# Loading the sinks and the identity after the first activations in a streaming encoder step

## The chip, the cores and the metric

The kernel runs on one core of one Trainium2 chip. The metric is the time of one execution on the device in microseconds (us), lower is better. Before the change three runs gave 2082.37, 2082.21 and 2081.52 us, with a median of 2082.21 us.

## The reference

The program computes one inference step of a small hybrid encoder. The input is a prompt of 2048 tokens and a sample of 32 tokens, both with 1024 features. Layer 0 is a gated DeltaNet layer. Layer 1 is a sliding-window attention layer with a learned sink for each head, and both share one K and V. All arithmetic is in float32. What matters for the start of the program is the first projection:

```python
def delta_layer(x, conv_buf, s0, w_in, conv_w, a_log, dt_bias, norm_w, w_out, ln_g, ln_b):
    proj = x @ w_in                                   # 1024 -> 4096 + 16 features
    qkv, new_buf = causal_conv(proj[..., :CONV_DIM], conv_buf, conv_w)
    a_in = proj[..., CONV_DIM + A_VW:CONV_DIM + A_VW + A_HEADS]
    b_in = proj[..., CONV_DIM + A_VW + A_HEADS:]
    ...

def sink_softmax(s, sinks):                           # in layer 1 only
    sk = sinks.astype(jnp.float32)[..., None, None]
    m = jnp.maximum(s.max(-1, keepdims=True), sk)
    p = jnp.exp(s - m)
    return p / (p.sum(-1, keepdims=True) + jnp.exp(sk - m))
```

The sinks enter in the attention of layer 1, the second half of the program. The identity matrix is an operand of the transposes on TensorE, of which the first stands behind the first projections.

## The kernel before, in words

**Stages.** `program` (L2273) runs the parts one after the other: `P1` is the input projection of layer 0 with its short convolution, `Delta` the recurrence, `O1` the output projection with its layer norm, `P2` the projections of layer 1, `Attention` the rest. `make_consts` (L2426) runs ahead of all of them and fills constants that several parts use.

**How a projection is done.** A float32 operand is split into two parts of a shorter format: `hi` is a rounded copy (a cast on ACT), `lo` is the raw value less `hi` (a subtraction on DVE or POOL). A product takes three matmuls: hi by hi (L79), lo activations by hi weights (L80), hi activations by lo weights (L81). Activations come transposed in five blocks of 416 tokens (`NB`, `TB`), and one block has eight slices `k` of 128 features. Weights come in blocks of 128 output features.

**The first block.** `P1.__init__` loads `wab_raw`, the weights of 16 small gate features, on ACT's DMA queue, and then the activations (L136). Block 0 comes in four pieces `q` of two slices each, 128x832, 416 KB. Pieces 0 and 2 go through SP's queue, 1 and 3 through ACT's. Blocks 1 to 4 come in two pieces of four slices each, 128x1664, 832 KB. Piece by piece ACT casts to `act_hi` (L70) and DVE subtracts to `act_lo` (L71). The raw pieces lie in four buffers (two under each of two tags), so that a later piece of the same tag can only be loaded when DVE has subtracted an earlier one. Between blocks 0 and 1 the program text asks for the first two weight blocks (`fetch_weights`, L48, `split_fetched`, L55 and L56). There is one buffer for raw weights, so the second is loaded when the first has been split.

**What follows.** `P1.qkv` (L150) takes each activation block in turn: sixteen gate matmuls (L166 with `act_hi`, L168 with `act_lo`, in order of `k`), then the 48 matmuls of the two weight blocks. The gate rows are transposed with the identity (L174).

**What sets the order.** In this part the program text doesn't set the order of the instructions on an engine. A scheduler of the build does, with a time model of its own, and it also gives each DMA, in the order in which it places them, one of eight completion semaphores, DMAHW0 to DMAHW7. SP's and ACT's queues share the eight. A DMA that gets a semaphore waits until the earlier DMA with that semaphore has landed. Each engine works strictly through its own list: an instruction that waits holds everything behind it, and DMA issues on ACT stand in the same list as ACT's casts. Later stages are written under `manual_schedule`, where the text's own order holds.

Of the kernel before, what the change touches and what calls it, by code (L numbers as in the profile page):

```python
# [36 lines left out]
def new_pool(tc, es, name, bufs=1, space=None, side=None):  # L37
    kw = {"reuse_waits": "tile"}
    if side is not None:
        kw["side"] = side  # L40
    if space is not None:
        kw["space"] = space
    return es.enter_context(tc.tile_pool(name=name, bufs=bufs, **kw))
# [16 lines left out]
def split_weights(nc, pool, src, sub):  # L60

    return split_fetched(nc, pool, fetch_weights(nc, pool, src), sub)


def split_acts(nc, res, b, raws, sub):

    h = res.tile([128, KC, TB], F32R, tag=f"act_hi{b}", name=f"act_hi{b}")
    l = res.tile([128, KC, TB], F32R, tag=f"act_lo{b}", name=f"act_lo{b}")
    for s, raw in raws:
        nc.scalar.copy(h[:, s, :], raw)  # L70
        sub.tensor_tensor(out=l[:, s, :], in0=raw, in1=h[:, s, :], op=ALU.subtract)  # L71
    return h, l
# [25 lines left out]
class P1:  # L98
# [4 lines left out]
    def __init__(self, tc, left, right, mid, I, O, T, G):  # L103
        self.tc, self.nc, self.I, self.O, self.T, self.G = tc, tc.nc, I, O, T, G
        nc = tc.nc
        self.resl = new_pool(tc, left, "p1_resl", 1, side="left")
        self.wp = new_pool(tc, left, "p1_w", 2, side="left")
        self.ppl = new_pool(tc, left, "p1_psl", 2, PSUM, side="left")
        self.resr = new_pool(tc, right, "p1_resr", 1, side="right")
        self.big = new_pool(tc, mid, "p1_big", 2, side="right")  # L110
        self.one = one = new_pool(tc, mid, "p1_one", 1, side="right")
        self.ppr = new_pool(tc, right, "p1_psr", 4, PSUM, side="right")
        self.pt = new_pool(tc, mid, "p1_pt", 2, PSUM, side="right")
        self.turn = 0
        self.convw = one.tile([128, 24, 4], F32, tag="convw", name="convw")
        self.convs = one.tile([128, 24, 3], F32, tag="convs", name="convs")
        self.convo = one.tile([128, 24, 6], F32, tag="convo", name="convo")
        self.sel = one.tile([128, 4, 128], F32, tag="sel", name="sel")
        self.nwh = self.resl.tile([128, 1], F32, tag="nwh", name="nwh")
        raw = one.tile([128, KC, 16], F32, tag="th", name="wab_raw")  # L120
        wab = one.tile([128, KC, 48], F32R, tag="parts", name="wab")
        nc.scalar.dma_start(raw[:], I["w_ab"])
        nc.scalar.copy(wab[:, :, 0:16], raw[:])
        nc.vector.tensor_tensor(out=wab[:, :, 32:48], in0=raw[:], in1=wab[:, :, 0:16], op=ALU.subtract)
        nc.gpsimd.memset(wab[:, :, 16:32].bitcast(F32), 0.0)
        self.wab = wab
        self.x = []
        for b in range(NB):
            if b == 1:
                self.w0 = [split_weights(nc, self.wp, I["w_in"][i], (nc.vector, nc.gpsimd)[i]) for i in range(2)]  # L130
            raws = []
            step = 2 if b == 0 else 4
            for q in range(KC // step):
                raw = self.big.tile([128, step, TB], F32, tag="Ry"[q % 2], name="act_raw")
                s = slice(q * step, q * step + step)
                (nc.sync if q % 2 == 0 else nc.scalar).dma_start(raw[:], I["xT"][b][:, s, :])  # L136
                raws.append((s, raw[:]))
            self.x.append(split_acts(nc, self.resr if b < 3 else self.resl, b, raws, nc.vector))
        nc.sync.dma_start(self.convw[:], I["conv_w"])
        nc.sync.dma_start(self.convs[:], I["conv_state"])  # L140
        nc.sync.dma_start(self.nwh[:], I["norm_w"])
        nc.scalar.mul(self.nwh[:], self.nwh[:], 0.5)
        nc.sync.dma_start(self.sel[:], I["sel"])

    def ps(self):
        self.turn += 1
        return (self.ppl if self.turn % 3 == 0 else self.ppr).tile([128, 512], F32, tag="ps", name="ps")
# [2278 lines left out]
def make_consts(tc, I, pool):  # L2426
    nc = tc.nc
    G = {}
    G["ident"] = pool.tile([128, 128], F32, tag="ident", name="ident")
    nc.sync.dma_start(G["ident"][:], I["ident"])  # L2430
    raw = pool.tile([128, 12], F32, tag="sinks", name="sinks")
    for i in range(2):
        nc.sync.dma_start(raw[i * 64:i * 64 + 64, 0:8], I["sinks"][i].partition_broadcast(64))
    for i in range(4):
        nc.sync.dma_start(raw[i * 32:i * 32 + 32, 8:12], I["sinks_s"][i].partition_broadcast(32))
    G["sinks"] = pool.tile([128, 12, 2], F32, tag="twice", name="twice")
    nc.vector.tensor_copy(G["sinks"][:], raw[:].unsqueeze(2).to_broadcast([128, 12, 2]))
    for name in ("hn", "eq", "ekd", "egl", "ngc"):
        G[name] = pool.tile([128, NTT, H], F32, tag=name, name="t_" + name)
    return G  # L2440
# [135 lines left out]
```

## Time and profile before

| | |
|---|---|
| median of three runs | 2082.21 us (2081.52 to 2082.37) |
| the profiled execution | 2085.37 us |
| its span, first to last instruction | 2083.6 us |
| PE (TensorE matmul) busy | 2025.9 us, 97% of the span |
| DVE, ACT, POOL busy | 1481.4, 993.3, 917.7 us |
| first matmul starts | 11.79 us into the span |

The profiled execution is 1.77 us longer than its span, which is what lies before the first and after the last instruction, and 3.16 us longer than the median run. In the rows of the profile PE is TensorE's matmuls, PEld its weight loads, ACT is ScalarE, DVE is VectorE, POOL is GpSimd. SPq and ACTq are the DMA issues of the two queues. In a row of the timeline the first number is the start in us from the span's start and the second the time it took, x2 stands for several merged instructions, and square brackets give the idle time of the engine before it with what ended it. In a row of stretches (windows) stand the length, busy time and instruction count of each engine, the granted clock, the share of time that the 16 DMA engines were busy, and their rate.

### The profile page before, as it was taken

To read this page: it belongs to the slowest core of one execution; us is meant where nothing else is said; L and a number is where in the kernel's file an instruction comes from. 1 tells how busy PE (TensorE), PEld (TensorE's weight loads), DVE (VectorE), ACT (ScalarE), POOL (GpSimd) and SP (SyncE) were. 2 spreads that over 40 slices of the span, in tenths; PEclk is the share of its full clock that TensorE was granted. 3 is DMA by queue.
4 is the path that set the end of the run, shared out by engine and by line. 5 is a ranking of instruction groups with operands and counts; after the bars stand their busy time and mean duration, and the time that the engine had idled before them with its cause. 6 is when DMAs were issued, how large, how long until landed. Compare 5 with 4: busy or idle time off the path is not lost.

```text
span 2083.6 us, 36939 instructions
## 1 busy us (share of the span) xinstructions
PE 2025.9 (97%) x13518; PEld 1856.4 (89%) x13518; DVE 1481.4 (71%) x2580; ACT 993.3 (48%) x2445; POOL 917.7 (44%) x1248
## 2 busy tenths in 40 slices
PE   7999999999999999999989998999989998999998
PEld 5999999999999999999888887899989997777775
DVE  4477666675556778888987897877878755666665
ACT  4354444446532266777763222534634445555552
POOL 0322213222222157777860113386255523566665
PEclk9999999999999999999999999899999999999999
DMA  5132333236756645555864999888767679434321
GB/s 209 29 96 81 100 112 103 92 98 201 215 162 200 190 134 175 166 170 166 302 226 117 270 244 258 264 249 292 261 217 239 202 211 305 112 107 112 102 73 66
DMA packets 355542, 360.82 MB, mean 173 GB/s; under 512 B 157585, under 2 KB 280241, under 8 KB 355345
## 3 DMA queue, kind: packets, MB, share of 16 engines
q1 hardware_dynamic: 348880, 344.03, 53.8%
q10 hardware_dynamic: 6480, 14.44, 2.0%
q8 instruction: 106, 1.74, 0.3%
q14 instruction: 76, 0.61, 0.1%
HBM read 235.54 MB, written 134.06 MB: 177 GB/s over the span
## 4 chain that ended last, share of the span: by engine, by line
PE 79%; DMA 8%; DVE 6%; issue 2%; POOL 2%; ACT 1%; SPq 1%; DVEq 0%; ACTq 0%; POOLq 0%
PE ps L79 12%; PE ps L81 12%; PE ps L80 11%; PE ot L1133 3%; PE ot L1134 3%; PE ot L1135 3%; PE S L2026 2%; PE ot L2059 2%; PE tr L2041 2%; PE X L1684 2%; PE X L1682 2%; PE X L1683 2%; PE g L695 1%; DMA w_raw<-in_b_w 1%; PE ks L846 1%
## 5 line engine op out<-in xcount | busy, mean ns | idle before, releaser
L79 PE MATMUL ps<-act_hi,w_hi 128*128 128x416 f32 x1280 | 455.2, 356 | 0.4 <-ACT w_hi L55 0.4
L81 PE MATMUL ps<-act_hi,w_lo 128*128 128x416 f32 x1280 | 450.3, 352 | 0.0
L80 PE MATMUL ps<-act_lo,w_hi 128*128 128x416 f32 x1280 | 448.2, 350 | 0.0
L79 PEld LDWEIGHTS ps<-act_hi,w_hi 128*128 128x128 f32 x1280 | 240.3, 188 | 4.5 <-ACT w_hi L55 0.7
L80 PEld LDWEIGHTS ps<-act_lo,w_hi 128*128 128x128 f32 x1280 | 240.7, 188 | 3.1
L81 PEld LDWEIGHTS ps<-act_hi,w_lo 128*128 128x128 f32 x1280 | 240.2, 188 | 3.2
L209 DVE SCALAR_TENSOR_TENSOR y<-R,convw,y 128x2083 f32<-128x2083 f32 x72 | 182.9, 2541 | 62.5 <-ACT y L206 46.7
L56 POOL TENSOR_TENSOR w_lo<-w_raw,w_hi 128x1024 fp32r<-128x1024 f32 x25 | 71.3, 2854 | 329.8 <-ACT w_hi L55 302.5
L729 POOL TENSOR_TENSOR tm<-L,Tt 128x60 f32<-128x60 f32 (+19 forms) x365 | 134.3, 368 | 80.6 <-issue 39.6
L1860 POOL TENSOR_TENSOR P<-e,sm 128x384 f32<-128x384 f32 (+2 forms) x128 | 102.3, 820 | 119.5 <-DVE sm L1850 113.3
L731 POOL TENSOR_TENSOR Tt<-Tt,tm 128x60 f32<-128x60 f32 (+19 forms) x365 | 138.5, 380 | 28.6
L1846 ACT ACTIVATE e<-S,nm 128x193 f32<-128x193 f32 (+2 forms) x260 | 104.6, 415 | 96.4 <-DVE nm L1841 57.6
L1355 DVE TENSOR_TENSOR w_lo<-w_raw,w_hi 128x512 fp32r<-128x512 f32 x132 | 139.0, 1069 | 10.7 <-ACT w_hi L1367 5.4
L305 ACT COPY R<-ps 128x416 f32<-128x416 f32 (+1 forms) x144 | 60.3, 442 | 106.8 <-PE ps L81 91.6
L1510 ACT ACTIVATE o<-X 128x416 f32<-128x416 f32 x80 | 41.4, 518 | 131.3 <-PE X L1684 128.7
L1133 PE MATMUL ot<-wo,g_hi 128*128 128x512 f32 x256 | 103.7, 405 | 0.0
L1134 PE MATMUL ot<-wo,g_hi 128*128 128x512 f32 x256 | 100.8, 394 | 0.0
L1135 PE MATMUL ot<-wo,g_lo 128*128 128x512 f32 x256 | 100.8, 394 | 0.0
L1367 ACT CAST w_hi<-w_raw 128x512 fp32r<-128x512 f32 x129 | 76.6, 615 | 18.3 <-POOL w_raw L1498 9.5
L215 DVE SCALAR_TENSOR_TENSOR y<-th,y 128x2083 f32<-128x2083 f32 x24 | 55.8, 2327 | 36.5 <-ACT th L213 36.5
L1841 DVE TENSOR_REDUCE nm<-S 128x4 f32<-128x772 f32 (+3 forms) x66 | 60.5, 917 | 15.2 <-PE S L2026 15.2
L213 ACT ACTIVATE th<-y 128x2083 f32<-128x2083 f32 x24 | 46.7, 1947 | 47.0 <-DVE y L209 43.7
(369 smaller groups left out, 5229.0 us busy)
## 6 DMA issues: line engine op xcount, KB each, us to landing
w_raw<-in_b_w SPq DMA_DIRECT2D x60, 512.0 KB
w_raw<-in_w_in SPq DMA_DIRECT2D x40, 512.0 KB
act_raw<-s_hT SPq DMA_DIRECT2D x64, 208.0 KB
s_rows<-o SPq DMA_DIRECT2D x50, 208.0 KB
k<-s_k SPq DMA_DIRECT2D x17, 512.0 KB
E<-s_E SPq DMA_DIRECT2D x17, 512.0 KB
s_hT<-hT SPq DMA_DIRECT2D x65, 128.0 KB
s_bq<-s_rows SPq DMA_DIRECT2D x40, 208.0 KB
```

What stands on the lines that cost most here:

```text
L79: nc.tensor.matmul(ps, hi[:, k, :], xh[:, k, :], start=(k == 0), stop=False)
L80: nc.tensor.matmul(ps, hi[:, k, :], xl[:, k, :], start=False, stop=False)
L81: nc.tensor.matmul(ps, lo[:, k, :], xh[:, k, :], start=False, stop=(k == KC - 1))
L209: nc.vector.scalar_tensor_tensor(out=y[:], in0=R[:, j:j + W], scalar=self.convw[:, i, j:j + 1], in1=y[:], op0=ALU.mult, op1=ALU.add)
L729: P.tensor_tensor(out=tm[:n, i0 - k:, :w], in0=L[:n, i0:, j:j + 1].to_broadcast(sh), in1=Tt[:n, j:j + 1, :w].to_broadcast(sh), op=ALU.mult)
L731: P.tensor_tensor(out=Tt[:n, i0:, :w], in0=Tt[:n, i0:, :w], in1=tm[:n, i0 - k:, :w], op=ALU.subtract)
L1133: nc.tensor.matmul(ps[:n], ghi[:, k, :n], hi, start=a, stop=False)
L1134: nc.tensor.matmul(ps[:n], ghi[:, k, :n], lo, start=False, stop=False)
L1135: nc.tensor.matmul(ps[:n], glo[:, k, :n], hi, start=False, stop=z)
L1355: P.tensor_tensor(out=lo, in0=raw, in1=hi, op=ALU.subtract)
L1846: self.nc.scalar.activation(x.e[:, h, u, :x.n], x.S[:, h, u, :], AF.Exp, bias=x.nm[:, h, u:u + 1], scale=1.0, accum_out=x.sm[:, h, u:u + 1])
L1860: self.nc.gpsimd.tensor_tensor(out=x.P[:, u, :nj * 128].rearrange("r (j h k) -> r j h k", h=2, k=64), in0=x.e[:, :, u, :n].rearrange("r h ...
```

## The change

The load of the identity is taken from `make_consts` and placed behind the text that loads activation block 0 and ahead of the first weight blocks. The six loads of the sinks (2 of 64x8 values, 4 of 32x4 values, each one row of memory copied to many partitions) and the copy on DVE that doubles them become a function, which is called at the end of `P1.__init__`, behind all activations and the small constants. Nothing else is edited, and the number of instructions of each kind stays.

```diff
@@ P1.__init__
                 (nc.sync if q % 2 == 0 else nc.scalar).dma_start(raw[:], I["xT"][b][:, s, :])
                 raws.append((s, raw[:]))
             self.x.append(split_acts(nc, self.resr if b < 3 else self.resl, b, raws, nc.vector))
+            if b == 0:
+                nc.sync.dma_start(G["ident"][:], I["ident"])
         nc.sync.dma_start(self.convw[:], I["conv_w"])
         nc.sync.dma_start(self.convs[:], I["conv_state"])
         nc.sync.dma_start(self.nwh[:], I["norm_w"])
         nc.scalar.mul(self.nwh[:], self.nwh[:], 0.5)
         nc.sync.dma_start(self.sel[:], I["sel"])
+        G["load_sinks"]()
@@ make_consts
-    nc.sync.dma_start(G["ident"][:], I["ident"])
     raw = pool.tile([128, 12], F32, tag="sinks", name="sinks")
-    for i in range(2):
-        nc.sync.dma_start(raw[i * 64:i * 64 + 64, 0:8], I["sinks"][i].partition_broadcast(64))
-    for i in range(4):
-        nc.sync.dma_start(raw[i * 32:i * 32 + 32, 8:12], I["sinks_s"][i].partition_broadcast(32))
     G["sinks"] = pool.tile([128, 12, 2], F32, tag="twice", name="twice")
-    nc.vector.tensor_copy(G["sinks"][:], raw[:].unsqueeze(2).to_broadcast([128, 12, 2]))
+
+    def load_sinks():
+        for i in range(2):
+            nc.sync.dma_start(raw[i * 64:i * 64 + 64, 0:8], I["sinks"][i].partition_broadcast(64))
+        for i in range(4):
+            nc.sync.dma_start(raw[i * 32:i * 32 + 32, 8:12], I["sinks_s"][i].partition_broadcast(32))
+        nc.vector.tensor_copy(G["sinks"][:], raw[:].unsqueeze(2).to_broadcast([128, 12, 2]))
+
+    G["load_sinks"] = load_sinks
```

The edit also makes the scheduler order the opening anew. From the gate matmuls of activation block 3 on PE has the same list as before, and the other engines have it from a few instructions behind the last split of block 4, with line numbers 2, 3 or 6 higher. Three places differ. Names carry a buffer number, which the build gives anew: `act_raw_130`, 132, 134 and 136 of before are pieces 0 to 3 of block 0, as `act_raw_122`, 124, 126 and 128 are now. `w_raw_148` and `w_raw_154` of before, now `w_raw_141` and `w_raw_147`, are the first and the second weight block.

SP's queue at the start of the program, before:

```order
L2430 DMA ident_79<-in_ident 128x128
L2433 DMA sinks_81<-in_sinks 64x8 x2
L2435 DMA sinks_81<-in_sinks_s 32x4 x2
L2435 DMA sinks_81<-in_sinks_s 32x4 [waits DMAHW0_49]
L2435 DMA sinks_81<-in_sinks_s 32x4 [waits DMAHW1_49]
L136 DMA act_raw_130<-in_xT 128x832 [waits DMAHW2_49]
L136 DMA act_raw_134<-in_xT 128x832 [waits DMAHW3_49]
L48 DMA w_raw_148<-in_w_in 128x1024 [waits DMAHW4_49]
```

and now:

```order
L136 DMA act_raw_122<-in_xT 128x832
L136 DMA act_raw_126<-in_xT 128x832
L140 DMA ident_79<-in_ident 128x128
L48 DMA w_raw_141<-in_w_in 128x1024
L141 DMA convw_111<-in_conv_w 128x96
```

Seven issues are gone from ahead of the two activation pieces, and neither the pieces nor the weights wait for a semaphore.

SP's queue further on, between the four small constants and the second weight block, now:

```order
L136 DMA act_raw_153<-in_xT 128x1664 [waits DMAHW3_49,DVE_49]
L2438 DMA sinks_80<-in_sinks 64x8 [waits DMAHW4_49]
L136 DMA act_raw_163<-in_xT 128x1664 [waits DMAHW5_49,DVE_49]
L2438 DMA sinks_80<-in_sinks 64x8 [waits DMAHW6_49]
L2440 DMA sinks_80<-in_sinks_s 32x4 [waits DMAHW0_49]
L2440 DMA sinks_80<-in_sinks_s 32x4 [waits DMAHW1_49]
L2440 DMA sinks_80<-in_sinks_s 32x4 [waits DMAHW3_49]
L2440 DMA sinks_80<-in_sinks_s 32x4 [waits DMAHW4_49]
L155 DMA triu_205<-in_triu 128x128 [waits DMAHW5_49]
L48 DMA w_raw_147<-in_w_in 128x1024 [waits DMAHW6_49,DVE_49]
```

The six sinks loads now stand between the first halves of blocks 1 and 2 (`act_raw_153`, `act_raw_163`) and the second weight block. The third small sinks load waits for the semaphore of `act_raw_153`, and `triu`, a small constant, for that of `act_raw_163`. Before, `triu` and another small load stood ahead of `act_raw_160`, a third between it and `act_raw_170` (the two halves, as they are called there), and the weight block one load behind `act_raw_170`.

ACT's list, which holds casts and DMA issues, before:

```order
L70 CAST act_hi0_138<-act_raw_132 128x832 [waits DMAHW3_49]
L70 CAST act_hi0_138<-act_raw_136 128x832 [waits DMAHW5_49]
L136 DMA act_raw_162<-in_xT 128x1664 [waits DVE_49]
L136 DMA act_raw_172<-in_xT 128x1664 [waits DMAHW7_49,DVE_49]
L70 CAST act_hi0_138<-act_raw_130 128x832 [waits DMAHW2_49]
L70 CAST act_hi0_138<-act_raw_134 128x832 [waits DMAHW3_49]
L55 CAST w_hi_150<-w_raw_148 128x1024 [waits DMAHW4_49]
```

and now:

```order
L70 CAST act_hi0_130<-act_raw_122 128x832 [waits DMAHW1_49]
L70 CAST act_hi0_130<-act_raw_126 128x832 [waits DMAHW2_49]
L70 CAST act_hi0_130<-act_raw_124 128x832 [waits DMAHW3_49]
L70 CAST act_hi0_130<-act_raw_128 128x832 [waits DMAHW5_49]
L136 DMA act_raw_155<-in_xT 128x1664 [waits DMAHW7_49,DVE_49]
L55 CAST w_hi_143<-w_raw_141 128x1024 [waits DMAHW6_49]
```

Before, ACT cast pieces 1, 3, 0, 2 and issued two loads of later blocks (the second halves of blocks 1 and 2) in between. Now it casts 0, 2, 1, 3, and one such load, the second half of block 1, stands ahead of the first weight cast.

On PE the gate matmuls of block 0 and the first weight block on block 0 stand in the same order. Behind them blocks 1 and 2 are now taken by halves, and the first matmul with the second weight block has 92 matmuls ahead of it instead of 74.

## The prediction

> **What bounds the kernel now.** I read the page first, its busy times and the summary of the chain of waits.
>
> ```profile
> PE 2025.9 (97%) x13518; PEld 1856.4 (89%) x13518; DVE 1481.4 (71%) x2580; ACT 993.3 (48%) x2445; POOL 917.7 (44%) x1248
> PE 79%; DMA 8%; DVE 6%; issue 2%; POOL 2%; ACT 1%; SPq 1%; DVEq 0%; ACTq 0%; POOLq 0%
> ```
>
> PE is the bound: it idles 2083.6 - 2025.9 = 57.7 us in all. What the edit can give back must lie in that idle time, or in matmuls that run slowly. The busy times by stretch say where the idle time is.
>
> ```profile
> 0.00:11.80 11.80, 0.01 (x1) 0.05 (x1) 2.60 (x5) 4.23 (x5) 0.68 (x9) 1.00 0.70 210
> 11.80:17.70 5.90, 5.44 (x16) 2.66 (x17) 4.05 (x4) 3.52 (x3) 0.00 (x0) 1.00 0.97 357
> 17.70:56.20 38.50, 36.32 (x186) 30.84 (x186) 16.59 (x26) 15.66 (x18) 2.85 (x5) 1.00 0.45 163
> 56.20:500.00 443.80, 443.80 (x2358) 433.58 (x2357) 296.11 (x217) 196.44 (x291) 115.45 (x104) 1.00 0.32 97
> ```
>
> The columns behind the length are PE, PEld, DVE, ACT, POOL. The opening up to 56.2 us idles 11.8 + 0.5 + 2.2 = 14.4 us, and the 444 us behind it idle nothing. So PE's end moves by as much as the opening gets shorter, as far as later waits follow PE. Next I read the timeline of the opening for all engines.
>
> ```profile
> 0.74 0.39 SPq L2430 DMA_DIRECT2D ident<-in_ident  x1
> 2.44 1.98 SPq L2435 DMA_DIRECT2D sinks<-in_sinks_s  x4
> 4.86 0.82 SPq L136 DMA_DIRECT2D act_raw<-in_xT  x2
> 1.17 0.46 ACTq L136 DMA_DIRECT2D act_raw<-in_xT  x1
> 2.98 0.36 ACTq L136 DMA_DIRECT2D act_raw<-in_xT  x1
> 5.03 0.88 ACT L70 CAST act_hi<-act_raw 128x832 fp32r<-128x832 f32 x1 [1.77 <-DMA act_raw<-in_xT]
> 8.18 0.88 ACT L70 CAST act_hi<-act_raw 128x832 fp32r<-128x832 f32 x1 [2.26 <-DMA act_raw<-in_xT]
> 10.80 1.92 ACT L70 CAST act_hi<-act_raw 128x832 fp32r<-128x832 f32 x2 [1.74 <-DMA act_raw<-in_xT]
> 11.79 0.55 PE L166 MATMUL ps<-act_hi,wab 128*48 128x416 f32 x1 [11.79 <-ACT act_hi L70]
> ```
>
> Matmuls need slices 0 and 1 first, and these are in piece 0, which SP issues only at 4.86 behind the identity and six sinks loads. Pieces 0 and 2 land last, and their casts begin at 10.80. PE starts when the first of them is done. Behind the start PE is slow:
>
> ```profile
> 12.80 0.53 PE L168 MATMUL ps<-act_lo,wab 128*16 128x416 f32 x1 [0.46 <-DVE act_lo L71]
> 16.59 0.55 PE L166 MATMUL ps<-act_hi,wab 128*48 128x416 f32 x1
> 16.94 0.55 PE L168 MATMUL ps<-act_lo,wab 128*16 128x416 f32 x1
> 17.71 0.35 PE L79 MATMUL ps<-act_hi,w_hi 128*128 128x416 f32 x1
> 17.90 0.35 PE L80 MATMUL ps<-act_lo,w_hi 128*128 128x416 f32 x1
> ```
>
> Up to about 17.3 a matmul starts every 0.35 us, later every 0.19 us, although the profile's granted clock reads 1.00 throughout. The first weight block is ready when PE gets to it at 17.71. Two waits remain behind that:
>
> ```profile
> 25.50 0.37 PE L168 MATMUL ps<-act_lo,wab 128*16 128x416 f32 x1 [1.62 <-DVE act_lo L71]
> 31.53 0.46 PE L79 MATMUL ps<-act_hi,w_hi 128*128 128x416 f32 x1 [0.37 <-ACT w_hi L55]
> 18.71 0.54 SPq L48 DMA_DIRECT2D w_raw<-in_w_in  x1
> 30.42 1.05 ACT L55 CAST w_hi<-w_raw 128x1024 fp32r<-128x1024 f32 x1 [3.74 <-DMA w_raw<-in_w_in]
> ```
>
> The first is for block 1's low part, the second for the second weight block, which takes 11.7 us from issue to cast.
>
> **The change part by part.** *Removed from the front.* SP's seven issues fill 0.74 to 4.86. Now piece 0 is issued where the identity was, 4.12 us earlier, piece 2 about 0.4 us after it (two took 0.82), and ACT issues its second piece right behind the first. When do all four land? They are 4 x 416 KB, with the 64 KB of gate weights 1.77 MB.
>
> ```profile
> 2.00:5.00 3.00, 0.00 (x0) 0.00 (x0) 0.29 (x1) 1.25 (x2) 0.00 (x0) 1.00 0.65 182
> 5.00:8.00 3.00, 0.00 (x0) 0.00 (x0) 1.02 (x1) 0.88 (x1) 0.00 (x0) 1.00 0.92 205
> 8.00:11.00 3.00, 0.00 (x0) 0.00 (x0) 1.20 (x2) 1.08 (x2) 0.00 (x0) 1.00 0.88 324
> 11.00:14.00 3.00, 1.76 (x5) 0.83 (x6) 2.05 (x2) 1.69 (x3) 0.00 (x0) 1.00 0.98 382
> 4.00:6.00 2.00, 0.00 (x0) 0.00 (x0) 0.05 (x1) 0.88 (x1) 0.00 (x0) 1.00 0.47 158
> act_raw<-in_xT SPq DMA_DIRECT2D x2, 416.0 KB
> w_raw<-in_w_in SPq DMA_DIRECT2D x40, 512.0 KB
> ```
>
> Hardly anything moves before 2.0. At the early rates (about 193 GB/s) 1.77 MB takes 9.2 us, to 11.2; at the later ones (about 353) 5.0 us, to 7.0. I take 280 GB/s, between the two, so 8.3: the engines were only 0.47 busy from 4 to 6, in a pause while small loads and late pieces came, and four full pieces stand in the queues now.
>
> *The split of block 0.* All four pieces must be cast and subtracted.
>
> ```profile
> L71 DVE TENSOR_TENSOR act_lo<-act_raw,act_hi 128x832 fp32r<-128x832 f32 x4 | 4.1, 1024 | 4.5 <-ACT act_hi L70 4.5
> L70 ACT CAST act_hi<-act_raw 128x832 fp32r<-128x832 f32 x4 | 3.5, 885 | 5.9 <-DMA act_raw<-in_xT 5.8
> 13.88 1.05 ACT L55 CAST w_hi<-w_raw 128x1024 fp32r<-128x1024 f32 x1 [1.16 <-DMA w_raw<-in_w_in]
> 14.96 1.23 DVE L56 TENSOR_TENSOR w_lo<-w_raw,w_hi 128x1024 fp32r<-128x1024 f32 x1 [1.19 <-ACT w_hi L55]
> ```
>
> Piece 0 should land near 5, as ACT's first did. Pieces 2, 1, 3 follow each other: cast of piece 2 from about 7.9 to 8.8, then three subtractions of 1.02, with a little between them, to 11.9. Three gate matmuls at 0.35 remain, to 13.0. In ACT's list the first weight cast now stands behind a load of block 1 that waits for the subtraction of piece 1, at 10.9: issue 0.35, cast 1.05 to about 12.35, subtraction 1.23 behind that of piece 3, to 13.6. The weights' 0.5 MB should have landed by then, 1.5 us behind the pieces. PE's third weight matmul may wait 0.25. So what began at 17.71 begins in effect at 13.25: **-4.45 us**.
>
> *Slow matmuls.* Before, the slow rate ended 4.5 us after PE began without pause (12.80 to 17.3). Now the dense run begins near 10.9, with the subtraction of piece 1, and ends slow at 15.4: 2.15 us of the weight matmuls run at 0.35 instead of 0.19, which loses 2.15 x (1 - 0.19/0.35) = **+1.0 us**, between 0 and 2.
>
> *The two waits behind.* Block 1 now comes by halves. Its first half is issued near 9, behind small constants, lands near 13.5 at 380 GB/s, and is split on ACT (1.58) and DVE (1.9) by about 18.3, when PE has finished weight block 1 on block 0; the first halves of blocks 1 and 2 follow at 1.9 us of DVE each while PE has 1.5 us of gate matmuls and 2.3 us of weight matmuls per half. I count +0.3 for what is left of the wait, and remove its 1.62. The second weight block is issued behind the landing of block 2's first half, near 17. PE asks for it after 92 matmuls, near 28, so its 0.37 falls too. Together **-2.0 + 0.3 us**.
>
> *What is added.* No instruction is. The doubling copy of the sinks (0.2 us on DVE) and the six loads move behind block 0, where PE has work in hand; the sinks are read in the attention, over 1000 us later. The identity is needed near 18 and lands with the pieces. All this I cost at nothing; with the cover gone, the six loads would cost their 3.2 us of issue on SP.
>
> **Sum:** -4.45 + 1.0 - 2.0 + 0.3 = -5.15 us. The profiled execution of 2085.37 (span 2083.6 and 1.77 around it) becomes 2080.2; it lies 3.16 above the median, so the median 2082.21 becomes 2077.1. Its own range: pieces at 7.0 give 1.3 more, no loss to slow matmuls 1.0, no new wait 0.3, and half a microsecond goes between executions (-8.2); pieces at 11.2 take 2.9 and 1.0 more of slow matmuls (-1.2), and something for new waits. That is 2074 to 2081.8.
>
> **The rivals.** *The bytes decide (2079.3).* If the early rate of about 193 GB/s is what the memory gives, the last piece lands at 11.2, and 2.9 of the gain stay out: -2.2. But only the two waits then go, and the start hardly moves; I allow 0.7 of the slow matmuls to be saved as the dense run starts late, so -2.9, no change by the bound below. For it: 5 to 8 us was 0.92 busy at 205 GB/s. Against: the 0.47.
>
> *PE stays slow longer (2079.9).* Early matmuls now come in bits: slices 0 and 1 near 6 to 8, a pause to about 9.7, bits to 11. If the dense run only counts from 13.25, the slow rate ends at 17.7, and all 24 matmuls of the first weight block on block 0 run at 0.35: 24 x 0.16 = 3.8 instead of 1.0, so -2.35. Against: the pause of 1.62 before 25.50 didn't bring the slow rate back. The Trainium skill speaks against this change here: its page "TensorE: Matmul & The Clock Gate", Part 1, has the array at half rate until it was busy through a window of some 3.4 us, and at half rate again after such a window idle. By that rule the early bits do not warm the array but cost nothing either, and the slow time would be an estimated 3.4 to 6.8 us from 10.9. The trace's 4.5 us agrees with it.
>
> *The second weight block comes late (2084.9, slower).* It stands behind `triu`, which waits for block 2's first half. If the halves land no earlier than the same two did on SP,
>
> ```profile
> 25.10 1.58 ACT L70 CAST act_hi<-act_raw 128x1664 fp32r<-128x1664 f32 x1 [1.85 <-DMA act_raw<-in_xT]
> 35.12 0.35 PE L79 MATMUL ps<-act_hi,w_hi 128*128 128x416 f32 x1
> 56.22 0.35 PE L166 MATMUL ps<-act_hi,wab 128*48 128x416 f32 x1
> ```
>
> then the weights are issued at 25.1, take 11.7, and are cast at 37.9. PE begins its 93rd matmul at 35.12 now, by the order of the rows, and the 93rd of the new order would begin at 37.9: +2.7. It decides from a landing later than 34.0. For it: the semaphores tie small loads to large ones. Against: those 11.7 us were spent beside four other large pieces, of which two are issued later now.
>
> *The gain is lost later (2082.2).* PE has some 43 us of later idle time. Were part of it set by something that runs from the start on its own, it would grow. I see no such thing: the 444 us behind the opening are full.
>
> **How the numbers follow.** Forecast 0.65, bytes 0.18, slow PE 0.08, late weights 0.06, lost later 0.03. A measurement of this kernel tells about 0.2%, 4.2 us, from no change. Of the forecast's 0.65 some 0.61 gain more than that and 0.04 do not; bytes add 0.03 to faster, 0.14 to same and 0.01 to slower; slow PE is all same; late weights 0.02 same, 0.04 slower; the last 0.02 and 0.01. That makes faster 0.64, same 0.30, slower 0.06. The range 2073.8 to 2082.0 takes in the forecast's own range and the next two rivals.
>
> **What would show it.** In the changed profile: SP's first row is `act_raw` at 0.74; the last 128x832 cast begins near 10 and the last such subtraction ends near 11.9 (bytes: near 14.8); PE's first weight matmul starts near 13.0; the 0.35 spacing ends near 15.4 (slow PE: 17.7); no PE wait over 1 us between 20 and 56; the second weight cast comes before 27 (late weights: after 34). Gate matmuls of block 3 begin near 51 instead of 56.22. I am wrong if that point doesn't move, or if it moves and the end doesn't.

## The result, and the profile after

The changed kernel takes 2076.82 us (median of 12 runs, 2072.91 to 2080.67) beside 2082.55 us for the kernel before (12 runs, 2080.73 to 2088.29). The ratio is 0.9966 with a 95% interval of 0.9955 to 0.9977: 4.8 to 9.4 us less. A second comparison gave 2076.71 beside 2081.86, a ratio of 0.9974 (0.9964 to 0.9984). One run of the kernel before, in a later comparison, took 11320.12 us and is left out of every median and ratio here.

The page of the changed kernel, span and busy times:

```profile
span 2075.2 us, 36940 instructions
...
PE 2023.8 (98%) x13518; PEld 1853.7 (89%) x13518; DVE 1483.4 (71%) x2580; ACT 994.0 (48%) x2445; POOL 907.5 (44%) x1248
```

The span is 8.4 us shorter: PE is busy 2.1 us less and idles 51.4 us instead of 57.7. What the opening gave is read between two points that both kernels have, PE's start and the gate matmuls of block 3, from which on PE has the same list. Stretches up to there, of the kernel before:

```profile
0.00:17.70 17.70, 5.46 (x16) 2.71 (x17) 6.64 (x8) 7.75 (x8) 0.68 (x9) 1.00 0.79 259
17.70:56.22 38.52, 36.34 (x186) 30.84 (x186) 16.59 (x26) 15.66 (x18) 2.85 (x5) 1.00 0.45 163
```

and of the changed kernel, with the 444 us behind the opening:

```profile
0.00:17.70 17.70, 10.70 (x41) 6.89 (x41) 7.42 (x7) 9.23 (x11) 0.68 (x9) 1.00 0.87 321
17.70:49.09 31.39, 31.39 (x162) 26.58 (x161) 15.56 (x26) 13.86 (x16) 3.74 (x5) 1.00 0.45 166
50.40:494.00 443.60, 443.60 (x2357) 433.87 (x2356) 298.15 (x217) 197.00 (x293) 105.79 (x104) 1.00 0.32 98
4.00:6.00 2.00, 0.09 (x1) 0.12 (x1) 0.45 (x2) 1.08 (x2) 0.00 (x0) 1.00 1.03 413
6.00:8.00 2.00, 1.54 (x4) 0.36 (x4) 1.56 (x2) 1.61 (x2) 0.00 (x0) 1.00 1.06 421
```

PE's idle time up to that point falls from 12.24 + 2.18 = 14.42 us to 7.00 us, and its busy time rises from 41.80 to 42.09 us. Block 3 therefore begins 7.42 - 0.29 = 7.13 us earlier, at 49.09 instead of 56.22, and nothing idles in the next 444 us. The row from 4 to 6 us, whose counterpart was shown in the prediction, has 413 GB/s where the kernel before moved 158 GB/s. The timeline of the changed kernel (rows between those shown are left out):

```profile
0.73 0.87 SPq L136 DMA_DIRECT2D act_raw<-in_xT  x2
1.17 0.94 ACTq L136 DMA_DIRECT2D act_raw<-in_xT  x2
4.93 0.88 ACT L70 CAST act_hi<-act_raw 128x832 fp32r<-128x832 f32 x1
6.39 1.67 ACT L70 CAST act_hi<-act_raw 128x832 fp32r<-128x832 f32 x2 [0.58 <-DMA act_raw<-in_xT]
8.37 0.89 ACT L70 CAST act_hi<-act_raw 128x832 fp32r<-128x832 f32 x1 [0.31 <-DMA act_raw<-in_xT]
7.31 3.01 DVE L71 TENSOR_TENSOR act_lo<-act_raw,act_hi 128x832 fp32r<-128x832 f32 x3 [0.44 <-ACT act_hi L70]
5.91 0.55 PE L169 MATMUL ps<-act_hi,wab 128*48 128x416 f32 x1 [5.91 <-ACT act_hi L70]
9.33 0.53 PE L171 MATMUL ps<-act_lo,wab 128*16 128x416 f32 x1 [0.63 <-DVE act_lo L71]
12.42 0.55 PE L169 MATMUL ps<-act_hi,wab 128*48 128x416 f32 x1
12.77 0.44 PE L171 MATMUL ps<-act_lo,wab 128*16 128x416 f32 x1
13.05 0.35 PE L79 MATMUL ps<-act_hi,w_hi 128*128 128x416 f32 x1
22.25 1.05 ACT L55 CAST w_hi<-w_raw 128x1024 fp32r<-128x1024 f32 x1 [1.11 <-DVE twice L2441]
49.09 0.35 PE L169 MATMUL ps<-act_hi,wab 128*48 128x416 f32 x1
```

All four pieces are issued by 2.1, the last is cast from 8.37, and the last subtraction ends at 7.31 + 3.01 = 10.32 (before at 13.78). PE opens at 5.91 instead of 11.79 and reaches the first weight matmul at 13.05 instead of 17.71. That is 4.66 us; the other 2.47 come behind it.

### The profile page after: what moved, and what is told of

It is laid out like the page before. It is cut to its first block, busy times and chain, and to the rows that moved or that the text cites. A ratio compares the mean times of both kernels' runs of the same rounds, so it can differ in the third digit from the quotient of the medians.

```text
span 2075.2 us, 36940 instructions
## 1 busy us (share of the span) xinstructions
PE 2023.8 (98%) x13518; PEld 1853.7 (89%) x13518; DVE 1483.4 (71%) x2580; ACT 994.0 (48%) x2445; POOL 907.5 (44%) x1248
## 4 chain that ended last, share of the span: by engine, by line
PE 75%; DVE 8%; DMA 7%; issue 3%; POOL 2%; SPq 2%; ACT 2%; DVEq 0%; POOLq 0%; ACTq 0%
PE ps L79 12%; PE ps L81 12%; PE ps L80 12%; PE ot L1136 3%; PE ot L1137 3%; PE ot L1138 3%; PE S L2029 2%; PE ot L2062 2%; PE tr L2044 2%; PE X L1687 2%; PE X L1685 2%; PE X L1686 2%; DMA r<-in_x 2%; PE g L698 2%; DMA act_raw<-s_sums 1%
## 5 line engine op out<-in xcount | busy, mean ns | idle before, releaser
L56 POOL TENSOR_TENSOR w_lo<-w_raw,w_hi 128x1024 fp32r<-128x1024 f32 x25 | 62.6, 2503 | 320.7 <-ACT w_hi L55 295.4
```

## The experiments

Each kernel is an edit of the changed kernel (one of the kernel before, where that is said). A single run can't tell kernels a few microseconds apart, since twelve runs of one kernel spread over some 8 us. So what is compared first is a point of the opening that repeats: in two profiles of the changed kernel block 3 began at 49.09 and 49.29. (With the identity moved alone it repeated worse, which is told there.)

**The identity moved alone.**

```diff
-        G["load_sinks"]()            # end of P1.__init__
+    for i in range(2):               # make_consts, on SP, as before
+        nc.sync.dma_start(raw[i * 64:i * 64 + 64, 0:8], I["sinks"][i]...)
+    for i in range(4):
+        nc.sync.dma_start(raw[i * 32:i * 32 + 32, 8:12], I["sinks_s"][i]...)
```

(The copy on DVE goes back with them.)

> Only the identity's load is moved; the six sinks loads stay ahead of the activations. The theory is that what counts is when SP issues pieces 0 and 2 of activation block 0, and that all SP issues ahead of them cost alike, 0.4 to 0.6 us each. Then the first piece is issued near 4.4 instead of 4.86, the last 128x832 subtraction ends near 13.3 instead of 13.78, and the gate matmuls of block 3, at 56.22 before and 49.09 after the change, begin between 55 and 56. Rival: the 64 KB of the identity, which the DMA engines carry ahead of the pieces, are what cost; then they begin near 51 or earlier.

One run: 2078.77 us. The first weight matmul begins at 15.39, 2.3 us earlier than before, yet block 3 at 55.74, only 0.48 us earlier. The timeline of this kernel shows where the rest went:

```profile
4.02 1.59 SPq L136 DMA_DIRECT2D act_raw<-in_xT  x2
...
21.69 0.23 PE L176 MATMUL tp<-ident,abr 48*128 48x48 f32 x1 [1.13 <-DVE gtmp L178]
...
24.20 0.53 PE L170 MATMUL ps<-act_lo,wab 128*16 128x416 f32 x1 [1.77 <-DVE act_lo L71]
24.53 0.55 PE L168 MATMUL ps<-act_hi,wab 128*48 128x416 f32 x1
...
55.74 0.35 PE L168 MATMUL ps<-act_hi,wab 128*48 128x416 f32 x1
```

SP issues the pieces at 4.02 (before 4.86). PE then waits for block 1's low part, as it did before, and is slow again behind that; the stretch from 24 to 26 us has a granted clock of 0.53.

**The sinks moved alone.**

```diff
-            if b == 0:
-                nc.sync.dma_start(G["ident"][:], I["ident"])
     G["ident"] = pool.tile([128, 128], F32, tag="ident", name="ident")   # make_consts
+    nc.sync.dma_start(G["ident"][:], I["ident"])
```

> Only the sinks loads and their copy are moved; the identity stays first on SP. By the theory of issue times SP issues piece 0 near 1.2 instead of 0.73, the last 128x832 subtraction ends 0.3 to 0.8 later than 10.32, and the gate matmuls of block 3 begin between 49.1 and 50. By the rival (the identity's bytes ahead of the pieces) they begin near 54.

One run: 2078.91 us. SP issues the pieces at 1.18, the rate from 4 to 6 us is 404 GB/s, and block 3 begins at 48.94, as early as in the changed kernel. The timeline of this kernel:

```profile
10.04 0.89 ACT L70 CAST act_hi<-act_raw 128x832 fp32r<-128x832 f32 x1 [1.10 <-DVE act_lo L71]
...
48.94 0.35 PE L167 MATMUL ps<-act_hi,wab 128*48 128x416 f32 x1
```

The last subtraction ends at 11.99, 1.67 later than in the changed kernel and not the 0.3 to 0.8 that were expected: ACT's last cast comes behind the issue of a load of a later block, which waits for DVE. Block 3 doesn't begin later for it. With the sinks moved, the identity in front costs nothing that reaches this point: their move alone gives what the whole change gives.

**Both halves timed.** The single times of the last two, 2078.8 and 2078.9, don't follow block 3's start (55.74 and 48.94). So both were timed in rounds, to see whether the end of the program does.

> The kernel with the identity moved and the six sinks loads still in front, now timed in rounds. Its one profile had block 3's gate matmuls at 55.74, 0.48 us before the kernel before (56.22), but its single time was 2078.8, not to be told from the changed kernel's. Theory (what the end gains is what this point gains): the median is 0.3 to 1.0 us under the kernel before, a ratio of 0.9995 to 0.9999, and its interval holds 1. Rival (the end gains from something else than the opening, for instance from where the small loads stand later): it gains as much as the changed kernel, a ratio near 0.997 with 1 outside the interval.

> The kernel with the six sinks loads moved and the identity still in front, timed in rounds. Its one profile had block 3's gate matmuls at 48.94, 7.28 us before the kernel before. Theory: the median gains what the changed kernel gains, 4 to 7.5 us, a ratio of 0.9964 to 0.998. Rival (the end gains from something else than the opening): the gain is split between the two moves, about 0.9985 each.

The identity alone: 2081.75 us (12 runs) beside 2082.61 (17 runs), a ratio of 0.9989 (0.9980 to 0.9999), that is 0.2 to 4.2 us. In the profile of this comparison block 3 begins at 54.27, 1.95 us earlier than before. PE began the first weight matmul at 16.46, later than the 15.39 of the other profile, but waited 0.11 us where the other had 1.13, and was not slow again behind the same wait:

```profile
24.23 0.36 PE L170 MATMUL ps<-act_lo,wab 128*16 128x416 f32 x1 [1.76 <-DVE act_lo L71]
24.43 0.35 PE L168 MATMUL ps<-act_hi,wab 128*48 128x416 f32 x1
```

The sinks alone: 2077.82 us (7 runs), a ratio of 0.9965 (0.9953 to 0.9977), the changed kernel's gain, with block 3 at 49.01. The end follows block 3, and the rival that the gain arises elsewhere falls: the identity's interval lies apart from the sinks' and holds the 0.5 to 1.95 us of its two profiles. For the identity 0.9995 to 0.9999 was expected, with 1 inside the interval. That is the upper end of what was measured, and 1 is just outside.

**The sinks in front, but on POOL's queue.**

```diff
+    for i in range(2):               # make_consts
+        nc.gpsimd.dma_start(raw[i * 64:i * 64 + 64, 0:8], I["sinks"][i]...)
+    for i in range(4):
+        nc.gpsimd.dma_start(raw[i * 32:i * 32 + 32, 8:12], I["sinks_s"][i]...)
```

(The call at the end of `P1.__init__` is taken out.)

> The identity is moved as in the change, and the six sinks loads stay first in the program, but go through POOL's DMA queue, so that SP issues piece 0 at once. If only SP's issue time was lost before, the pieces come as after the change: last 128x832 cast begins near 8.4, first weight matmul near 13.0, gate matmuls of block 3 near 49.1. Rival: the small copies themselves hold up the transfers of the pieces (descriptor making or the DMA engines), whoever issues them; then the last cast begins 1.5 to 2.5 us later, and block 3 at 50.5 to 52.

One run: 2079.18 us, block 3 at 51.30. SP issues the pieces at 0.74, but the last cast begins 1.7 us later than in the changed kernel. The timeline of this kernel:

```profile
10.05 0.89 ACT L70 CAST act_hi<-act_raw 128x832 fp32r<-128x832 f32 x1 [1.05 <-DMA act_raw<-in_xT]
```

Its busy times from 6 to 8 us, and the DMA queue of POOL in that stretch (packets, MB, share of the 16 engines' time):

```profile
6.00:8.00 2.00, 1.54 (x4) 0.41 (x4) 1.05 (x2) 0.89 (x1) 0.00 (x0) 1.00 0.89 226
```

```profile
q0 software_dynamic: 49, 0.00, 24.9%
```

The rate is 226 GB/s where the changed kernel moves 421, and POOL's queue takes 24.9% of the DMA engines' time for 49 packets of almost no bytes. SP and ACT issue the four pieces here when the changed kernel does, by 2.1, so this delay is one of the transfers and not of the issue. The rival was right for POOL's queue, with both of its numbers: tiny loads on another queue slow the pieces. The whole costs less than with the loads on SP, where block 3 began at 54.27 and 55.74. What the transfers alone lose when the loads are on SP this kernel doesn't say.

**The sinks on SP, the pieces on ACT's queue.** Here no piece stands behind a sinks load on its queue.

```diff
-                (nc.sync if q % 2 == 0 else nc.scalar).dma_start(raw[:], I["xT"][b][:, s, :])
+                (nc.sync if q % 2 == 0 and b else nc.scalar).dma_start(raw[:], I["xT"][b][:, s, :])
```

(and the sinks in front on SP, as in the first experiment.)

> The six sinks loads stay first on SP, the identity is moved, and all four pieces of block 0 go through ACT's queue. Theory of the own queue: the small loads only hold up what stands behind them on SP. Then the pieces, issued by ACT between 1.2 and 5, are all cast by about 9.5, with the last 128x832 cast beginning before 8.8, and the first weight matmul comes near 13.5 because the weights still stand behind the small loads on SP. Rival: while small loads are issued, transfers of the other queue start late too, although the DMA engines are not busy (as ACT's second piece did before, which took 5.2 us from issue to cast). Then the last cast begins at 10 or later and the DMA share from 4 to 6 us stays under 0.7.

One run: 2075.53 us. ACT issues the four pieces at 1.15, 2.64 and 3.04 (two), all ahead of the 4.86 of before. The last three issues and the last cast in the timeline of this kernel, and its busy times from 4 to 6 us:

```profile
2.64 0.36 ACTq L136 DMA_DIRECT2D act_raw<-in_xT  x1
...
3.04 0.94 ACTq L136 DMA_DIRECT2D act_raw<-in_xT  x2
...
10.56 0.89 ACT L70 CAST act_hi<-act_raw 128x832 fp32r<-128x832 f32 x1 [0.22 <-DMA act_raw<-in_xT]
```

```profile
4.00:6.00 2.00, 0.29 (x1) 0.15 (x1) 0.35 (x1) 0.88 (x1) 0.00 (x0) 1.00 0.75 163
```

The last cast begins 2.2 us later than in the changed kernel, and the rate from 4 to 6 us is 163 GB/s, the 158 of before and not the 413 of after. The rival's number for the cast (10 or later) came true, the share of busy DMA engines is 0.75 and not under 0.7. But this doesn't show that SP's small loads hold up the transfers of ACT's queue, because the pieces were also issued later: the last at 3.53 where the changed kernel has 1.66. From its issue to the last of its semaphore events in the trace that piece took 7.0 us here and 6.7 there, so at most some 0.3 of the 2.2 us are left for slower transfers, and those went through one queue instead of two. ACT's second issue begins 0.03 us behind the landing of the gate weights (2.64 behind 2.61; in the kernel before 2.98 behind 2.95), while in the changed kernel it comes ahead of it (1.66 and 4.71). Presumably their cast stands ahead of it in ACT's list; the third and the fourth follow at once. Block 3 begins at 49.97, 6.25 us earlier than before, so most of the gain at that point is to be had without moving the sinks.

**The changed kernel without the sinks loads.**

```diff
     def load_sinks():
-        for i in range(2):
-            nc.sync.dma_start(raw[i * 64:i * 64 + 64, 0:8], I["sinks"][i]...)
-        for i in range(4):
-            nc.sync.dma_start(raw[i * 32:i * 32 + 32, 8:12], I["sinks_s"][i]...)
+        nc.vector.memset(raw[:], 0.0)
```

> As the change, but the sinks are not loaded at all: a fill with zeros on DVE takes their place, so the attention's sinks are zero. If the moved loads are hidden behind block 0, as the prediction costs them, nothing changes: first weight matmul near 13.05, gate matmuls of block 3 between 48.9 and 49.3. Rival: they cost in their new place through the semaphores that tie them to large pieces and hold SP's queue; then the second weight block is cast before 22.25 and block 3 begins 0.5 us or more before 49.09.

One run: 2073.44 us, within the range of the changed kernel's runs. The first weight matmul begins at 13.05, as in the changed kernel, block 3 at 48.82, 0.27 us earlier:

```profile
48.82 0.35 PE L169 MATMUL ps<-act_hi,wab 128*48 128x416 f32 x1
```

At their new place the loads cost at most 0.3 us there, about what two profiles of one kernel differ by (0.2).

**The loads doubled.** In the kernel before, the six sinks loads are made a second time, into a tile that is filled later anyway.

```diff
     nc.sync.dma_start(G["ident"][:], I["ident"])
+    G["hn"] = pool.tile([128, NTT, H], F32, tag="hn", name="t_hn")
+    for i in range(2):
+        nc.sync.dma_start(G["hn"][i * 64:i * 64 + 64, 0, 0:8], I["sinks"][i]...)
+    for i in range(4):
+        nc.sync.dma_start(G["hn"][i * 32:i * 32 + 32, 1, 0:4], I["sinks_s"][i]...)
```

> The kernel before with the six sinks loads made twice, the second time into a buffer that is filled later anyway: 13 small loads ahead of the pieces on SP. The scheduler moves the casts of pieces 0 and 2 behind two casts of blocks 1 and 2 on ACT. By issue times (0.5 to 0.6 us each) SP issues piece 0 near 8.2 and the first matmul starts between 14 and 16, 2.5 to 4 us later than 11.79; block 3's gate matmuls begin between 57 and 60. Rival: the wait for piece 0 is set by bytes and not by the issues ahead of it; then the first matmul starts before 13 and block 3 stays within 1 us of 56.22.

One run: 2096.04 us. Timeline of this kernel:

```profile
9.16 0.90 SPq L136 DMA_DIRECT2D act_raw<-in_xT  x2
...
11.88 1.58 ACT L70 CAST act_hi<-act_raw 128x1664 fp32r<-128x1664 f32 x1 [3.58 <-DMA act_raw<-in_xT]
...
19.90 1.67 ACT L70 CAST act_hi<-act_raw 128x832 fp32r<-128x832 f32 x2 [0.78 <-DMA w_raw<-in_w_in]
```

The pieces are issued at 9.16, 4.3 us later than before for six loads more. Of this 2.8 us are issues, 0.47 each, and the rest is waiting between them. The start moves by more: the first matmul begins at 20.88 (before 11.79) and block 3 at 67.49 (11.3 us later), both outside what was expected. The scheduler put the 128x1664 casts of blocks 1 and 2, which wait for their loads, ahead of the last two casts of block 0 on ACT. The direction is right, the size is not that of the loads alone.

**PE warmed up.** Twenty-four small matmuls on zeros at the start, ahead of any data.

```diff
         self.turn = 0
+        zero = one.tile([128, 256], mybir.dt.bfloat16, tag="triu", name="zero")
+        nc.vector.memset(zero[:], 0.0)
+        warm = self.pt.tile([128, 512], F32, tag="tp", name="warm")
+        for _ in range(24):
+            nc.tensor.matmul(warm[:, 0:256], zero[:, 0:128], zero[:], start=True, stop=True)
```

> The changed kernel with 24 matmuls of 128x256 on zeros ahead of everything on PE, whose result nobody reads. They keep PE busy from about 1 us until near 6. Theory: the 0.35 us spacing of the first matmuls is a slow rate of PE that ends after some 3 to 5 us of work, whatever the work is. Then the 16 gate matmuls of block 0 run at 0.19, the first weight matmul starts near 11 and the third waits for the weights' low part until about 12.15, and block 3's gate matmuls begin near 47.9 instead of 49.09; the time falls by some 1.2 us, less than the rounds can tell. Rival: the spacing belongs to the gate matmuls (their narrow weights) and not to a rate; then they stay at 0.35, the first weight matmul starts near 13.05, and nothing moves.

2073.92 us (6 runs, 2072.32 to 2077.07) beside 2081.86, a ratio of 0.9966 (0.9954 to 0.9979). Timeline of this kernel:

```profile
1.05 0.82 PE L119 MATMUL warm<-zero 128*128 128x256 bf16 x3 [1.05 <-DVE zero L116]
...
7.12 0.35 PE L174 MATMUL ps<-act_hi,wab 128*48 128x416 f32 x1
7.31 0.35 PE L176 MATMUL ps<-act_lo,wab 128*16 128x416 f32 x1
...
11.40 0.35 PE L79 MATMUL ps<-act_hi,w_hi 128*128 128x416 f32 x1
...
47.83 0.35 PE L174 MATMUL ps<-act_hi,wab 128*48 128x416 f32 x1
```

The same gate matmuls that start every 0.35 us in the changed kernel up to 12.9 start every 0.19 us here from 6.92 on. So the slow rate belongs to the time that PE has worked, not to this form of matmul. The traces agree: their record of the granted clock begins where the 0.35 us spacing ends, at 17.39 us in the kernel before, at 12.94 in the changed kernel and at 3.69 here. Block 3 begins 1.26 us earlier than in the changed kernel's profile.

**The changed kernel again**, in the same comparison as the last:

> The changed kernel once more, beside the kernel before on the same chip. Its opening should be the same to 0.2 us (first matmul near 5.9, gate matmuls of block 3 near 49.1). If what differs between executions lies in the stages with many transfers, 1000 to 1700 us, the shift against the profile of before stays at 7.1 us up to 900 us and then moves by up to 3 us either way, and the time ratio comes out between 0.9955 and 0.9977. Rival: part of the gain is lost again later in every execution; then the shift shrinks by over 1 us at the same place as in another profile of this kernel.

2076.71 us (12 runs, 2072.56 to 2082.70), block 3 at 49.29. How the shift went on behind it is told in the next section. The warmed-up kernel's median is 2.8 us under this, but the intervals of the two ratios overlap, so it is the best tried and not shown to be better.

## Why the prediction was right, step by step

The forecast was 2077.1 us with 5.15 us gained; measured were 2076.82 and, by medians, 5.73. The mechanism held: pieces that are issued first land earlier, PE starts earlier, and the end follows. Inside it, the opening gave 7.13 us where the sum had 5.15, by these steps.

*The pieces land at 8.3, at 280 GB/s.* The landing held: the last cast, which waits for its DMA, begins at 8.37. The rate held as an average only, of little at first and 413 to 421 GB/s from 4 to 8 us. The bytes rival fails there: the early 158 to 205 GB/s was no limit of the memory, as 413 GB/s with the same pieces shows.

*Split by 11.9, first weight matmul in effect at 13.25 (-4.45).* The last cast was said to begin near 10 and began at 8.37, and the last subtraction ended at 10.32, 1.6 earlier. The sum let pieces 2, 1 and 3 all come near 8; pieces 2 and 1 landed at 6.37 and 6.69 (by the trace's semaphore events), so that one cast and two subtractions were left when piece 3 came at 8.35. PE began the weights at 13.05, near the 13.0 that was said, and this is partly luck: where the sum had three gate matmuls left behind the last subtraction there were eight, one every 0.35 us. The two misses cancel: -4.66 instead of -4.45.

*Slow matmuls (+1.0).* This term was mis-sized. The sum let the dense run begin at 10.9 and stay slow to 15.4. It began at 9.33 and was slow until 12.9, 3.6 us later, so no weight matmul was slow in this profile (two were in the second, where it lasted until 13.5), and PE's busy time up to block 3 rose by only 0.29. The loss fell on the gate matmuls instead, inside the step above; what it costs in all the warmed-up kernel shows, 1.26 us at block 3. The slow-PE rival, with 17.7 for the end, fails too. The length is not fixed: 4.5 us in the kernel before, and with the sinks moved alone it ended 4.2 us after the dense start in one profile and 2.4 in the other. The Trainium skill, "TensorE: Matmul & The Clock Gate", Part 1, has a window of some 3.4 us that runs freely, whatever the kernel does, so that the length varies; lengths of 2.4 to 4.8 us over these kernels and the warm-up's effect agree with that.

*The later waits (-2.0 + 0.3).* Both are gone and nothing came for them: 31.39 of 31.39 us are busy from 17.70 to 49.09. The +0.3 was not there. Some 0.2 us of smaller waits, which the sum had not counted, went too, and the 186 matmuls from the first weight matmul to block 3 are busy 36.04 us instead of 36.33. In all 2.47 behind the first weight matmul.

*Moved loads at nothing.* Right within the 0.3 us of the kernel without them. The second weight block, said to be cast before 27, was cast at 22.25 in spite of `triu`, so the late-weights rival fails.

*What the 444 us do.* The shift of 7.13 us at block 3 stood at 7.11 to 7.13 up to about 920 us of the program. From 1000 to 1720 us, where more is loaded and stored, it wandered between 3.3 and 8.2 and ended at 8.4; with the second profile of the changed kernel it was 6.93, then between 3.5 and 7.2, and ended at 9.9. In both it shrank by 3 to 4 us up to 1040, as the rival of the second comparison has it, but stood at 6.5 and 6.8 again by 1100, so that most of this is no loss.

Part of the wandering is PE's clock: the traces have stretches of 3.4 us with a granted clock of 0.50, partly at other places in each execution (at 1082 in the kernel before, at 1030 and 1010 in the two profiles of the changed kernel). The second profile of the identity moved alone shows what one of them costs: a stretch from 743.3 to 746.7, which the kernel before doesn't have, took the shift from 1.95 to 0.42. So the later part differs between executions by some microseconds. Whether some of the 7.1 is lost there stays open. The medians give 5.73 and 5.15, the means of the same runs 6.94 and 5.39, and the two intervals, 4.8 to 9.4 and 3.3 to 7.5 us, both hold 7.1 and neither holds 0, so the rival that the gain is lost later falls. That the forecast of 5.15 lies nearer to the medians than the opening's own gain is luck: it came of terms counted too dearly and not of a reason why the end should keep less.

## What to carry to other kernels

Look at what stands ahead of the first large load on its queue, and let tiny loads that are read late go behind it; the gain stays as long as the bounding engine is full behind the opening (here 7.1 us up to about 920 us). A kernel whose order a scheduler makes has to be read again after the edit: moving one load out of seven brought the first weight matmul 1.3 to 2.3 us forward and block 3 by 0.5 to 2 us, and six added loads, which delayed the pieces by 4.3 us, cost 11. Compare such kernels at a point of the opening, and let rounds confirm the end, since single runs spread over more than the gain.

## What the runs showed of the hardware that was not expected

- Six broadcast loads of 0.5 and 2 KB on POOL's queue slowed large transfers on SP's and ACT's queues that were issued at the same times as without them: 226 GB/s from 6 to 8 us instead of 421, with 49 packets of POOL's queue taking 24.9% of the DMA engines' time. Their cost was expected on their own queue alone. For the same loads on SP's queue the runs don't separate this from the later issue of the large ones.
- PE went slow again for 3.4 us (24.2 to 27.6) behind waits of 1.13 and 1.77 us in one profile of the identity moved alone, with a granted clock of 0.53, and not in the other, which had the wait of 1.76 alone. At the start of the program the rows of stretches print 1.00 over the same 0.35 us spacing, because the trace's record of the granted clock begins only where that spacing ends (17.39 us in the kernel before, 12.94 in the changed kernel). So there the spacing has to be read, and a short stretch of lost clock can be one execution's own.
